# Conditioning groups as a low-priority stream on the Vector engine, own tables per layer, and token halves further apart in a two-layer diffusion trunk

## The chip, the cores and the metric

The kernel runs on one core of a Trainium2 chip. The metric is the device time of one execution in microseconds (us). A core has TensorE (PE; its weight loads are shown as PEld), VectorE (DVE), ScalarE (ACT), GpSimd (POOL) and SyncE (SP, which issues nearly all DMAs here). Each engine takes its instructions in the order in which the kernel wrote them.

## The reference, cut to what matters

Two layers over 256 latent tokens ("half 0", segment 0) and 256 context tokens ("half 1", segment 1), model width 1024, all in float32. The context is only an input to layer 1, so layer 1 computes half 0 alone in most places.

```python
for l in range(2):
    m  = silu(c)     @ ada_w[l] + ada_b[l]     # conditioning: 6 x 1024 for latent tokens
    mc = silu(c_ctx) @ ada_w[l] + ada_b[l]     # the same for context tokens
    h  = rms_norm(x, g0) * (1 + sc1) + sh1     # "modulate"
    y  = token_mix(h, hc, ...)                 # projection, branches A B C D, gated merge, out-projection w_o
    x  = x + g1 * rms_norm(y, g)               # "residual"
    h  = rms_norm(x, g2_) * (1 + sc2) + sh2
    x  = x + g2 * rms_norm(conv_ffn(h), g)     # up 1024 -> 2 x 2816, conv of width 3, gate, down
    # with l == 0 the same for the context: xc, hc, sh1c, ...
```

The merge is the sum over four branches of sigmoid(gate) * (branch @ w_br), then @ w_o.

## The kernel before

Every weight matrix is used in full float32 precision by splitting it into a high part in fp32r (a cast on ACT, `wh`) and a low part (a subtraction on DVE, `wl`); each product is three matmuls (high-high, high-low, low-high). `plan_layer` lists the weights in order, 1024 elements by 128 partitions each; `w_dma` loads them into NRAW raw buffers, `split_gen` splits them into NW pairs, `take` hands out the next, `drop` gives one back. A weight is 24 matmuls against 512 token columns, or against 256 where one half alone is computed.

Order: the program writes all engines' instructions in one order that a model of the engines' clocks decides on (`Model`, `Flow`). The main line writes TensorE's projections (`chunks`). After every three matmuls `Flow.poll` lets side generators write their next steps if what they wait for is ready by the model: first evacuations of results (`post`), then the norm chain of half 0 (`chain`), then splits of weights, then the streams in the order of STREAMS: `chain2` (norm chain of half 1), `pv`, `main` (attention, retention), `aux`, `fill` (convolution taps and tables). A stream takes a step only while DVE and ACT are, by the model, at most its limit ahead of TensorE (0.3 to 3 us). `Flow.until(cond)` polls until a condition holds; `idle_work` (conditioning on TensorE) is advanced only in such a loop. Waits in this order bind the order of instructions, not the engines: an engine on the chip waits only for data, buffers and what stands before it in its own queue.

PSUM has 8 banks; CAP says how many the main stream ("m"), scores and norms ("s"), transposes ("t") and retention or attention values ("v") may hold. Temporaries are 60 tiles (NT) of 128x512 float32 that all streams share.

Conditioning: each layer has 12 groups of 512 outputs (0, 1 shift; 2, 3 scale; 4, 5 gate; 6, 7 shift, 8, 9 scale, 10, 11 gate of the feed-forward). A group is made on TensorE (`ada_gen`: 8 loads of 256 KB, 8 products, 4 transposes, `adp`, `adt`) or on DVE (`ada_stream`: per 128 outputs two loads of 256 KB, and a multiply-and-reduce for each half of the 1024 inputs and each of the two vectors, `adw`, `adj`). Groups 0 to 3 of layer 0 run on TensorE at the start. Before the change the others were placed so: layer 0, groups 4 to 9 on DVE in stream `aux` beside the last merge (branch C), with all of `aux` written out before the out-projection; 10 and 11 on TensorE as idle work in the out-projection; layer 1, groups 0 and 2 as idle work before the feed-forward of layer 0, 1 and 3 on DVE in it, 4 to 6 as idle work in its last down-projection; 7 to 9 on DVE beside layer 1's last-but-one merge and the last, 10 and 11 as idle work in layer 1's out-projection.

Stages of layer 0 in the trace: projections and attention to 303 us, merge D 303 to 371, `proj_c` (projections of branch C) to 438, merge A with retention beside it to 529, merge C to 594, out-projection (`op`), feed-forward (`f`, `fa`, `fb`; down-projections also named `op`) from 677 to 1054. In `project` the last output chunks (`tail` of them) are computed for half 0 first and for half 1 after, with their weights held, so that half 0's norm chain (`residual`, `modulate`, tiles `rt`, `xs`, `q`, `ht`, `hh`, `hl`) runs under half 1's matmuls. The feed-forward then starts with four weights against half 0 and the same against half 1.

Of the kernel before, what the change touches and what calls it, by code (L numbers as in the profile page):

```python
# [8 lines left out]
F32 = mybir.dt.float32  # L9
# [6 lines left out]
KD = 8  # L16
# [128 lines left out]
class Flow:  # L145
# [7 lines left out]
    STREAMS = (("chain2", 3.0, 1), ("pv", 3.0, 1), ("main", 1.5, 2), ("aux", 1.5, 1), ("fill", 0.3, 1))  # L153
# [90 lines left out]
def trunk_kernel(  # L244
# [67 lines left out]
    CAP = {"m": 4, "s": 4, "t": 2, "v": 1}  # L312
# [22 lines left out]
    cst_sb = const.tile([128, 640], F32, name="cst_sb")  # L335
# [19 lines left out]
    CC = cst_sb[:, 384:512].rearrange("p (t d) -> p t d", t=2)  # L355
    SS = cst_sb[:, 512:640].rearrange("p (t d) -> p t d", t=2)
# [7 lines left out]
    ada = const.tile([128, 48, 2], F32, name="ada")  # L364
    gain = const.tile([128, 4, KD, 2], F32, name="gain")
    ada_next = const.tile([128, 16, 2], F32, name="ada_next")
    gain_next = const.tile([128, KD, 2], F32, name="gain_next")
# [42 lines left out]
    def tables_gen():  # L410
        yield (row_sb, vec_sb, cst_sb)
        act.copy(identr, ident)
        act.copy(masks, cst_sb[:, 128:384].rearrange("p (t d) -> p t d", t=2))
        for l in range(2):
            yield from layer_tables(l)
        finish_decays()
# [151 lines left out]
    def ada_gen(l, j, raw, nxt=False, h=None):  # L568
# [19 lines left out]
        o = (ada_next if nxt else ada)[:, c0:c0 + nc_, :]  # L588
# [8 lines left out]
        if idx is not None:  # L597
# [3 lines left out]
                out=(gain_next[:, ks, :] if nxt else gain[:, idx, ks, :]), in0=o,  # L601
# [5 lines left out]
    def c_rows_gen(vecs, rows_):  # L607

        for v in vecs:
            r = [tmp("crow") for _ in range(2)]  # L610
            for h in range(2):
                dma.dma_start(out=r[h], in_=c_b[:, v, 512 * h:512 * h + 512])
            rows_[v] = r
        for v in vecs:
            for h in range(2):
                t = rows_[v][h]
                yield (t,)
                th = tmp("crth")
                act.activation(out=th, in_=t, func=AF.Tanh, scale=0.5)
                yield (th,)  # L620
                dve.scalar_tensor_tensor(out=t, in0=th, scalar=1.0, in1=t, op0=ALU.add, op1=ALU.mult)

    def ada_stream(l, js, nxt=False, vecs=(0, 1)):

        A, G = (ada_next, gain_next) if nxt else (ada, gain)
        half_c = lambda c, h: ada_t[l, c, :, 512 * h:512 * h + 512]

        def load(c):
            r = [tmp("adw") for _ in range(2)]
            for h in range(2):  # L630
                dma.dma_start(out=r[h], in_=half_c(c, h))
            return r

        c_rows = {}
        yield from c_rows_gen(vecs, c_rows)
        cs = [4 * j + i for j in js for i in range(4)]
        raw = load(cs[0])
        for n_, c in enumerate(cs):
            cur, raw = raw, load(cs[n_ + 1]) if n_ + 1 < len(cs) else None
            for v in vecs:  # L640
                yield (cur[0], cur[1], c_rows[v][0], c_rows[v][1])
                a = small(1, "adc")
                for h in range(2):
                    junk = cur[h] if v == vecs[-1] else tmp("adj")
                    dve.tensor_tensor_reduce(
                        out=junk, in0=cur[h], in1=c_rows[v][h], scale=0.5,
                        scalar=(a if h else vec_sb[:, l, V_ADAB + c:V_ADAB + c + 1]), op0=ALU.mult, op1=ALU.add,
                        accum_out=(A[:, c, v:v + 1] if h else a),
                    )
                    yield  # L650
            if c % 4 == 3:
                c0 = c - 3
                kind, k0 = divmod(c0, 8)
                idx = {1: 0, 2: 1, 4: 2, 5: 3}.get(kind)
                w = slice(vecs[0], vecs[-1] + 1)
                if idx is not None:
                    ks = slice(k0, k0 + 4)
                    ng = vec_sb[:, l, V_NORM + 8 * idx + k0:V_NORM + 8 * idx + k0 + 4]
                    dve.scalar_tensor_tensor(
                        out=(G[:, ks, w] if nxt else G[:, idx, ks, w]), in0=A[:, c0:c0 + 4, w],  # L660
                        scalar=(1.0 if idx in (0, 2) else 0.0),
                        in1=ng.unsqueeze(2).to_broadcast([128, 4, len(vecs)]), op0=ALU.add, op1=ALU.mult,
                    )
                ada_done.update((l, x) for x in range(c0, c0 + 4))
# [34 lines left out]
    def new_S(name):  # L699
        return tp.tile([128, 256], F32, tag="S", name=name, bufs=4)  # L700
# [5 lines left out]

    def modulate(which, s, b, ks=range(KD), nxt=False):
        sh0 = (0, 24)[which]
        A, G = (ada_next, gain_next) if nxt else (ada, gain[:, (0, 2)[which]])
        R = b[:, 0:256]  # L710
        prev = None

# [1148 lines left out]
```

## Time and profile before

| | |
|---|---|
| time, median of 3 runs (lowest to highest) | 1666.54 us (1664.19 to 1669.51) |
| the profiled execution: its time, its span | 1664.61 us, 1662.8 us |
| busy share of the span: PE, DVE, ACT, POOL | 96%, 75%, 48%, 2% |
| mean granted TensorE clock | 0.978 of full speed |
| conditioning loads: `in_ada_w` (for TensorE), `in_ada_t` (for DVE) | 104 and 88 of 256 KB |

The span is the time from the first to the last instruction of one profiled execution. Busy is the time in which an engine executes; a matmul's end is modelled, so matmuls overlap in the record, and how fast they follow one another is read from their starts or from how many lie in a stretch. The clock is the share of full speed that the chip granted TensorE in a stretch; its two levels are 1.2 GHz (0.5) and 2.4 GHz (1.0). A releaser is the instruction whose end ended a wait.

### The profile page before, as it was taken

To read this page: it belongs to the slowest core of one execution; us is meant where nothing else is said; L and a number is where in the kernel's file an instruction comes from. 1 tells how busy PE (TensorE), PEld (TensorE's weight loads), DVE (VectorE), ACT (ScalarE), POOL (GpSimd) and SP (SyncE) were. 2 spreads that over 40 slices of the span, in tenths; PEclk is the share of its full clock that TensorE was granted. 3 is DMA by queue.
4 is the path that set the end of the run, shared out by engine and by line. 5 is a ranking of instruction groups with operands and counts; after the bars stand their busy time and mean duration, and the time that the engine had idled before them with its cause. 6 is when DMAs were issued, how large, how long until landed. Compare 5 with 4: busy or idle time off the path is not lost.

```text
span 1662.8 us, 25016 instructions
## 1 busy us (share of the span) xinstructions
PE 1603.9 (96%) x9358; PEld 1346.4 (81%) x9358; DVE 1245.9 (75%) x2698; ACT 793.0 (48%) x1705; POOL 36.5 (2%) x38
## 2 busy tenths in 40 slices
PE   6999999999999995899999999899999999999998
PEld 3876776788778875688888888788687999899998
DVE  4666898994585998799547546789887899578876
ACT  3666466324323314454334324456665554556653
POOL 0000000000000000000000000000100000000000
PEclk9999999999999997899999999899999999889999
DMA  9421211223313586254322326244133368626552
GB/s 337 153 64 39 76 64 51 76 89 99 111 55 122 190 290 244 76 170 160 101 94 96 102 82 220 82 149 139 52 117 116 118 208 283 245 90 217 183 173 73
DMA packets 83561, 224.80 MB, mean 135 GB/s; under 512 B 9073, under 2 KB 17777, under 8 KB 83441
## 3 DMA queue, kind: packets, MB, share of 16 engines
q1 hardware_dynamic: 83152, 222.69, 40.1%
q8 instruction: 73, 1.20, 0.3%
q10 hardware_dynamic: 288, 0.52, 0.1%
q14 instruction: 48, 0.39, 0.1%
HBM read 222.13 MB, written 1.05 MB: 134 GB/s over the span
## 4 chain that ended last, share of the span: by engine, by line
PE 77%; issue 13%; DVE 5%; DMA 3%; ACT 1%; SPq 0%; POOL 0%; POOLq 0%; DVEq 0%; ACTq 0%
PE mg L129 16%; PE tm L129 11%; PE op L129 9%; PE mb L129 8%; PE fa L129 7%; PE fb L129 7%; PE pv L129 3%; PE sc L129 2%; PE cqk L129 2%; PE pa L129 2%; PE ptp L129 2%; PE pg L129 2%; PE csc L129 1%; DVE adj L129 1%; PE nrm L129 1%
## 5 line engine op out<-in xcount | busy, mean ns | idle before, releaser
L129 DVE TENSOR_TENSOR wl<-raw,wh 128x512 fp32r<-128x512 f32 (+1 forms) x624 | 405.1, 680 | 152.1 <-ACT wh L129 151.0
L129 ACT CAST wh<-raw 128x512 fp32r<-128x512 f32 (+1 forms) x624 | 358.3, 613 | 174.7 <-PE fb L129 46.0
L129 PE MATMUL mg<-hh,wh 128*128 128x512 f32 (+1 forms) x512 | 178.8, 349 | 0.0
L129 PE MATMUL mg<-hh,wl 128*128 128x512 f32 (+1 forms) x512 | 172.3, 336 | 0.0
L129 PE MATMUL mg<-hl,wh 128*128 128x512 f32 (+1 forms) x512 | 172.3, 336 | 0.0
L129 DVE SCALAR_TENSOR_TENSOR co<-zp,hdw,co 128x482 f32<-128x482 f32 (+29 forms) x240 | 129.3, 602 | 0.0
L129 PE MATMUL op<-gh,wh 128*128 128x256 f32 (+1 forms) x370 | 122.2, 330 | 0.0
L129 PE MATMUL op<-gh,wl 128*128 128x256 f32 (+1 forms) x370 | 121.4, 328 | 0.0
L129 PE MATMUL op<-gl,wh 128*128 128x256 f32 (+1 forms) x370 | 121.4, 328 | 0.0
L129 PE MATMUL tm<-wh,hh 128*128 128x512 f32 x272 | 112.0, 412 | 2.8 <-ACT hh L129 2.8
L129 PEld LDWEIGHTS mg<-hh,wh 128*128 128x128 f32 x512 | 97.1, 190 | 20.3 <-issue 11.4
L129 ACT ACTIVATE mth<-mg 128x512 f32<-128x512 f32 (+1 forms) x64 | 31.5, 491 | 170.0 <-PE mg L129 169.5
L129 PE MATMUL tm<-wh,hl 128*128 128x512 f32 x272 | 107.0, 393 | 1.9 <-DVE hl L129 1.9
L129 PE MATMUL fa<-hh,wh 128*128 128x512 f32 (+1 forms) x320 | 107.6, 336 | 0.0
L129 PE MATMUL fa<-hl,wh 128*128 128x512 f32 (+1 forms) x320 | 107.5, 336 | 0.0
L129 PE MATMUL fa<-hh,wl 128*128 128x512 f32 (+1 forms) x320 | 107.5, 336 | 0.0
L129 PE MATMUL fb<-hh,wh 128*128 128x512 f32 (+1 forms) x320 | 107.5, 336 | 0.0
L129 PE MATMUL fb<-hl,wh 128*128 128x512 f32 (+1 forms) x320 | 107.5, 336 | 0.0
L129 PE MATMUL fb<-hh,wl 128*128 128x512 f32 (+1 forms) x320 | 107.5, 336 | 0.0
L129 PE MATMUL tm<-wl,hh 128*128 128x512 f32 x272 | 106.6, 392 | 0.0
L129 PEld LDWEIGHTS mg<-hh,wl 128*128 128x128 f32 x512 | 97.1, 190 | 10.2
L129 PEld LDWEIGHTS mg<-hl,wh 128*128 128x128 f32 x512 | 97.3, 190 | 8.1
(259 smaller groups left out, 3685.5 us busy)
## 6 DMA issues: line engine op xcount, KB each, us to landing
raw<-in_w_fm SPq DMA_DIRECT2D x88, 512.0 KB, 3.5
raw<-in_f_up SPq DMA_DIRECT2D x88, 512.0 KB, 3.7
adw<-in_ada_w SPq DMA_DIRECT2D x104, 256.0 KB, 5.4
adw<-in_ada_t SPq DMA_DIRECT2D x88, 256.0 KB, 5.2
raw<-in_w_tm SPq DMA_DIRECT2D x40, 512.0 KB, 3.5
raw<-in_w_br SPq DMA_DIRECT2D x32, 512.0 KB, 3.5
raw<-in_f_d SPq DMA_DIRECT2D x32, 512.0 KB, 3.5
raw<-in_w_o SPq DMA_DIRECT2D x16, 512.0 KB, 4.0
```

The lines of the kernel that those rows point to most:

```text
L129: r = f(*a, **kw)
```

## The change

The conditioning on DVE becomes a stream of its own, `ada`, last in STREAMS with a limit of 0.3 us. It has four sets, each of which begins when a stage is reached: layer 0, groups 4 and 5 from merge D on; layer 0, groups 6 to 9 from merge A on; layer 1, groups 0 to 3 and (latent vector alone) 6 to 9 from the feed-forward of layer 0 on. In a set all first halves of the chunks come first, then all second halves, which add to what the first left in the table. Each layer has its own tables `ada` and `gain`. The main line waits for groups 4 and 5 ahead of `proj_c`, for 6 to 9 after merge C and for layer 1's two sets ahead of the last down-projection. On TensorE remain groups 10 and 11 of both layers, all as idle work of layer 0's out-projection, and groups 4 and 5 of layer 1. `tail` is 5 instead of 3, the feed-forward of layer 0 starts with six weights (three pairs, LEAD) against half 0, the main stream may hold 6 banks, and six split and four raw weights are buffered instead of five and five. The space for it comes from smaller constants (masks are loaded to a temporary) and three instead of four tiles `S`.

```diff
-IN_MERGE = ((4, 5, 6, 7, 8, 9), (7, 8, 9))
-IDLE = (((10, 11), (4, 5, 6)), ((10, 11), ()))
+IDLE = ((((0, 10), (0, 11), (1, 10), (1, 11)), ((1, 4), (1, 5))), ((), ()))
+ADA_SETS = (
+    ("merge D", 0, (4, 5), (0, 1)), ("merge A", 0, (6, 7, 8, 9), (0, 1)),
+    ("ffn", 1, (0, 1, 2, 3), (0, 1)), ("ffn", 1, (6, 7, 8, 9), (0,)),
+)
-NRAW = 5
+NRAW = 4
-NW = 5
+NW = 6
+LEAD = 3
-    STREAMS = (..., ("aux", 1.5, 1), ("fill", 0.3, 1))
+    STREAMS = (..., ("aux", 1.5, 1), ("fill", 0.3, 1), ("ada", 0.3, 1))
-    CAP = {"m": 4, "s": 4, "t": 2, "v": 1}
+    CAP = {"m": 6, "s": 4, "t": 2, "v": 1}
-    ada = const.tile([128, 48, 2], F32, name="ada")
-    ada_next = const.tile([128, 16, 2], F32, name="ada_next")
+    ada = [const.tile([128, 48, 2], F32, name=f"ada{l}") for l in range(2)]
...
+        for when, l, js, vecs in ADA_SETS:
+            yield (lambda: when in stage,)
+            cs = [4 * j + i for j in js for i in range(4)]
+            for h in range(2):
+                rows_ = [tmp("crow") for _ in vecs]
+                for v, r in zip(vecs, rows_):
+                    dma.dma_start(out=r, in_=c_b[:, v, 512 * h:512 * h + 512])
+                raw = load(l, cs[0], h)
+                for r in rows_:
+                    yield (r,)
+                    th = tmp("crth")
+                    act.activation(out=th, in_=r, func=AF.Tanh, scale=0.5)
+                    yield (th,)
+                    dve.scalar_tensor_tensor(out=r, in0=th, scalar=1.0, in1=r, op0=ALU.add, op1=ALU.mult)
+                for n_, c in enumerate(cs):
+                    cur, raw = raw, load(l, cs[n_ + 1], h) if n_ + 1 < len(cs) else None
+                    for v, r in zip(vecs, rows_):
+                        yield (cur, r)
+                        o = ada[l][:, c, v:v + 1]
+                        dve.tensor_tensor_reduce(
+                            out=(cur if v == vecs[-1] else tmp("adj")), in0=cur, in1=r, scale=0.5,
+                            scalar=(o if h else vec_sb[:, l, V_ADAB + c:V_ADAB + c + 1]), op0=ALU.mult, op1=ALU.add,
+                            accum_out=o,
+                        )
...
-            tail = 3 if last and full else 0
+            tail = 5 if last and full else 0
...
+            stage.add("merge D")
             merge(stD)
+            flow.until(ada_need(0, 4, 5))
             proj_c()
...
+            stage.add("merge A")
             merge(stA, there=lambda: not flow.q["fill"])
             flow.drain("main")
-            go("aux", ada_stream(l, IN_MERGE[l]))
             merge(stC, last=True)
+            flow.until(ada_need(0, 6, 7, 8, 9))
         else:
-            go("aux", ada_stream(l, IN_MERGE[l], vecs=(0,)))
...
-            for j in (0, 2):
-                flow.idle_work.append(ada_gen(1, j, ada_load(1, j), nxt=True))
...
             chunks(list(zip(banks, ws)), H, L, half(0), KD, pre=lambda k: need(k, (0,)))
-            for p in range(2):
+            for _ in range(2):
+                banks.append(bank("m", "f0"))
+                ws.append(take(8))
+                chunks([(banks[-1], ws[-1])], H, L, half(0), KD)
+            for p in range(LEAD):
                 up_pair(p, banks[2 * p:2 * p + 2], ws[2 * p:2 * p + 2], half(1), pre=lambda k: need(k, (1,)))
...
-            go("aux", ada_stream(1, (1, 3), nxt=True))
+            stage.add("ffn")
...
+            flow.until(ada_need(1, 0, 1, 2, 3, 6, 7, 8, 9))
+            for i in IDLE[l][1]:
+                flow.idle_work.append(ada_gen(*i, ada_load(*i)))
         down(2, ys)
...
+    flow.add("ada", ada_stream())
```

## Rows read from the trace of the kernel before

**Rows 1.** The page's first part, and one of its costliest groups.

```profile
span 1662.8 us, 25016 instructions
...
PE 1603.9 (96%) x9358; PEld 1346.4 (81%) x9358; DVE 1245.9 (75%) x2698; ACT 793.0 (48%) x1705; POOL 36.5 (2%) x38
...
L129 DVE TENSOR_TENSOR wl<-raw,wh 128x512 fp32r<-128x512 f32 (+1 forms) x624 | 405.1, 680 | 152.1 <-ACT wh L129 151.0
```

**Rows 2.** TensorE's waits, 600 to 660: us in all, times, longest.

```profile
PE op L129 <- DVE wl L129: 12.6, 1, 12.6
PE op L129 <- ACT wh L129: 9.2, 1, 9.2
```

**Rows 3.** ACT's waits in the same stretch.

```profile
ACT ys L129 <- DVE adc L129: 30.6, 1, 30.6
```

**Rows 4.** Windows by stage: length, each engine's busy us, clock, DMA share, GB/s.

```profile
303.00:362.00 59.00, 59.00 (x262) 48.56 (x262) 57.29 (x91) 16.22 (x30) 0.00 (x0) 1.00 0.29 98
...
372.00:438.00 66.00, 66.00 (x299) 54.84 (x298) 28.56 (x45) 26.39 (x45) 0.00 (x0) 1.00 0.33 109
438.00:529.00 91.00, 91.00 (x450) 72.76 (x449) 62.53 (x147) 27.79 (x51) 4.40 (x4) 1.00 0.22 74
529.00:594.00 65.00, 65.00 (x288) 53.81 (x288) 56.40 (x124) 24.01 (x43) 0.00 (x0) 1.00 0.59 195
594.00:621.00 27.00, 27.00 (x121) 22.36 (x120) 25.74 (x68) 1.77 (x3) 0.00 (x0) 1.00 0.92 330
621.00:644.00 23.00, 1.26 (x5) 0.54 (x3) 22.39 (x65) 8.15 (x19) 0.00 (x0) 0.56 0.56 207
...
715.00:802.00 87.00, 87.00 (x385) 72.08 (x384) 83.95 (x159) 41.69 (x70) 0.00 (x0) 1.00 0.48 158
802.00:1020.00 218.00, 218.00 (x963) 180.56 (x963) 114.88 (x176) 80.22 (x138) 0.00 (x0) 1.00 0.29 94
...
1438.00:1458.00 20.00, 16.06 (x88) 10.87 (x86) 12.19 (x34) 7.02 (x17) 2.37 (x2) 0.71 0.31 105
```

**Rows 5.** The same windows for tile `adw` alone: PE, PEld, DVE.

```profile
529.00:594.00 65.00, 0.00 (x0) 0.00 (x0) 26.46 (x36) 1.00 0.59 195
594.00:644.00 50.00, 0.00 (x0) 0.00 (x0) 42.92 (x60) 0.80 0.76 273
```

**Rows 6.** DVE's timeline, 600 to 606: start, us, instruction.

```profile
602.20 0.75 DVE L129 CUSTOM_DVE_ANT_0 adw<-adw,crow,vec_sb 128x512 f32<-128x512 f32 x1
...
602.99 0.75 DVE L129 CUSTOM_DVE_ANT_0 adw<-adw,crow,adc 128x512 f32<-128x512 f32 x1
...
603.67 0.75 DVE L129 CUSTOM_DVE_ANT_0 adj<-adw,crow,vec_sb 128x512 f32<-128x512 f32 x1
```

**Rows 7.** The chain of work, 360 to 380: start, us, what.

```profile
371.72 0.89 PE abc L129 x8
...
375.36 0.89 PE abc L129 x8
```

**Rows 8.** The chain of work around layer 0's feed-forward turn and its end.

```profile
644.02 12.38 PE op L129 x88
656.40 0.34 PE nrm L129 x4
...
664.19 0.35 PE nrm L129 x4
...
699.62 15.08 PE f L129 x96
...
1050.72 2.87 PE op L129 x24
```

**Rows 9.** TensorE's timeline, 674 to 679.

```profile
676.78 0.39 PE L129 MATMUL f<-hh,wh 128*128 128x256 f32 x1 [1.12 <-ACT hh L129]
```

**Rows 10.** TensorE's timeline, 1051 to 1074.

```profile
1053.86 1.07 PE L129 MATMUL adp<-adw,cS 128*32 128x512 f32 x8
...
1070.04 0.66 PE L129 MATMUL adt<-cst_sb,adsb 128*128 128x128 f32 x4 [2.28 <-ACT adsb L129]
...
1072.88 0.56 PE L129 MATMUL pg<-hh,wh 128*128 128x256 f32 x1
```

**Rows 11.** ACT's timeline, 1042 to 1075.

```profile
1065.12 0.91 ACT L129 ACTIVATE hh<-ht,ada_next 128x256 fp32r<-128x256 f32 x2 [3.02 <-DVE ht L129]
```

More of the change, by code (lines that the diff above doesn't have):

```diff
@@ L145 @@
 class Flow:
-    STREAMS = (("chain2", 3.0, 1), ("pv", 3.0, 1), ("main", 1.5, 2), ("aux", 1.5, 1), ("fill", 0.3, 1))
+    STREAMS = (("chain2", 3.0, 1), ("pv", 3.0, 1), ("main", 1.5, 2), ("aux", 1.5, 1), ("fill", 0.3, 1), ("ada", 0.3, 1))
     def __init__(self, model):
@@ L363, in trunk_kernel @@
     hh, hl = [None] * KD, [None] * KD
-    ada = const.tile([128, 48, 2], F32, name="ada")
-    gain = const.tile([128, 4, KD, 2], F32, name="gain")
-    ada_next = const.tile([128, 16, 2], F32, name="ada_next")
-    gain_next = const.tile([128, KD, 2], F32, name="gain_next")
+    ada = [const.tile([128, 48, 2], F32, name=f"ada{l}") for l in range(2)]
+    gain = [const.tile([128, 4, KD, 2], F32, name=f"gain{l}") for l in range(2)]
     def pair(name, shape):
@@ L412, in tables_gen @@
         act.copy(identr, ident)
-        act.copy(masks, cst_sb[:, 128:384].rearrange("p (t d) -> p t d", t=2))
+        mk = raw_masks.pop()
+        yield (mk,)
+        act.copy(masks, mk.rearrange("p (t d) -> p t d", t=2))
         for l in range(2):
@@ L600, in ada_gen @@
             dve.scalar_tensor_tensor(
-                out=(gain_next[:, ks, :] if nxt else gain[:, idx, ks, :]), in0=o,
+                out=gain[l][:, idx, ks, :], in0=o,
                 scalar=(1.0 if idx in (0, 2) else 0.0),
@@ L623, in ada_stream @@
[L623 to L664, printed above, removed]
@@ new lines, in trunk_kernel, with ada_stream, load @@
+    stage = set()
+    def ada_stream():
+        def load(l, c, h):
+            t = tmp("adw")
+            dma.dma_start(out=t, in_=ada_t[l, c, :, 512 * h:512 * h + 512])
+            return t
+        for when, l, js, vecs in ADA_SETS:
+            yield (lambda: when in stage,)
+            cs = [4 * j + i for j in js for i in range(4)]
+            for h in range(2):
+                rows_ = [tmp("crow") for _ in vecs]
[18 more added lines that the diff above has]
+                        )
+                    if h and c % 4 == 3:
+                        c0 = c - 3
+                        kind, k0 = divmod(c0, 8)
+                        idx = {1: 0, 2: 1, 4: 2, 5: 3}.get(kind)
+                        w = slice(vecs[0], vecs[-1] + 1)
+                        yield
+                        if idx is not None:
+                            ks = slice(k0, k0 + 4)
+                            ng = vec_sb[:, l, V_NORM + 8 * idx + k0:V_NORM + 8 * idx + k0 + 4]
+                            dve.scalar_tensor_tensor(
+                                out=gain[l][:, idx, ks, w], in0=ada[l][:, c0:c0 + 4, w],
+                                scalar=(1.0 if idx in (0, 2) else 0.0),
+                                in1=ng.unsqueeze(2).to_broadcast([128, 4, len(vecs)]), op0=ALU.add, op1=ALU.mult,
+                            )
+                        ada_done.update((l, x) for x in range(c0, c0 + 4))
@@ L705, in need, with modulate @@
         flow.until(lambda: all((s, k) in hready for s in segs))
-    def modulate(which, s, b, ks=range(KD), nxt=False):
+    def modulate(l, which, s, b, ks=range(KD)):
         sh0 = (0, 24)[which]
-        A, G = (ada_next, gain_next) if nxt else (ada, gain[:, (0, 2)[which]])
+        A, G = ada[l], gain[l][:, (0, 2)[which]]
         R = b[:, 0:256]
@@ L733, in modulate, with residual @@
         rest(*prev)
-    def residual(which, s, ys, b, Sx=None, sums=None):
+    def residual(l, which, s, ys, b, Sx=None, sums=None):
         R = b[:, 0:256]
@@ L768, in residual @@
             dve.scalar_tensor_tensor(
-                out=t, in0=ys[k][:, half(s)], scalar=gain[:, (1, 3)[which], k, s:s + 1], in1=R,
+                out=t, in0=ys[k][:, half(s)], scalar=gain[l][:, (1, 3)[which], k, s:s + 1], in1=R,
                 op0=ALU.mult, op1=ALU.mult,
@@ L787, in norm_chain @@
             b2 = bank("s", "nrm")
-            yield from residual(which, s, ys, b, sums=b2)
+            yield from residual(l, which, s, ys, b, sums=b2)
             added.add((l, which))
@@ L795, in norm_chain @@
             yield
-            yield from residual(which, s, ys, b, Sx)
+            yield from residual(l, which, s, ys, b, Sx)
             free(b)
@@ L1442, in final_feature @@
                 u = half_tmp("fu")
-                dve.tensor_scalar(out=u, in0=y, scalar1=gain[:, 3, m, 0:1], scalar2=None, op0=ALU.mult)
+                dve.tensor_scalar(out=u, in0=y, scalar1=gain[l][:, 3, m, 0:1], scalar2=None, op0=ALU.mult)
                 if m < KD - 1:
@@ L1694, in layer @@
             for p in range(p0, p0 + nk):
-                if p > 1:
+                if p >= (LEAD if full else 2):
                     up_pair(p)
@@ L1731, in start_chain @@
             yield (lambda: {(0, c) for c in (k, k + 1, 8 + k, 9 + k)} <= ada_done,)
-            yield from modulate(0, s, b, (k, k + 1))
+            yield from modulate(0, 0, s, b, (k, k + 1))
         free(b)
-    first = []
+    first, raw_masks = [], []
     for j, h in ((0, 0), (0, 1), (1, 0), (1, 1)):
```

38 lines of the change are left out of this document (12 added, 26 removed).

## The prediction

> **What bounds the kernel now.** I read the page's first part, then TensorE's waits, then the windows by stage, then the chain of waits and the timelines around the few places where TensorE stops. TensorE is busy 1603.9 of 1662.8 us [rows 1], so everything but TensorE's own stream is hidden, and a gain can only come from three sources: stretches where TensorE waits, stretches where it runs at the lower clock, and work that can be taken off it. One wait is large: in the out-projection of layer 0 it stands 9.2 us for a cast of ACT and then 12.6 us for a low half of DVE [rows 2]. ACT's own queue says why: a copy of the projection's result stood 30.6 us behind DVE's conditioning [rows 3], because its buffer came from that work, and the casts of weights stood behind that copy. The window 621 to 644 shows it: TensorE 1.26 of 23 us, DVE 22.39, clock 0.56 [rows 4]. The stage before it shows where it comes from: the conditioning of layer 0, groups 4 to 9, is 96 reduce instructions on DVE (24 chunks, 2 vectors, 2 halves), started with merge C at 529; 36 of them were through at 594, when that merge ended, and 60 came after it [rows 4, 5]. From 594 TensorE ran exactly the weights that were split ahead (5 x 5.44 = 27.2 us, at 87.00 us for 385 matmuls or 226 ns each, 24 to a weight [rows 4]), then stood.
>
> The smaller places are the turns from one sublayer to the next, where half 0 of the tokens goes through residual, norm and modulation while TensorE holds some half-1 work to cover it. Out-projection to feed-forward: half 0 ends near 656, half 1 near 664, the first matmul on new rows is at 676.8, the first on half 1 at 699.6 [rows 8, 9]. Layer 0 to 1: half 1 ends near 1053.9, the first `pg` comes at 1072.9 [rows 10]. Layer 1's own turn: 1438 to 1458 at clock 0.71 [rows 4].
>
> **The change, part by part.** The sum is against the profiled run (span 1662.8, 1664.61 us in all); the median shown is 1.9 us above that run, and I carry the difference over.
>
> *The stall after merge C (T1).* Groups 4 and 5 now go from merge D on, 6 to 9 from merge A on. The second set is 64 reduces. One that reads the accumulator just written starts 0.79 us after its predecessor, one that doesn't starts 0.68 after (602.20, 602.99, 603.67 [rows 6]). With the first halves of all chunks before the second halves none reads a fresh one, so the set is 64 x 0.68 = 43.5, and 46.2 with four preparations of vector rows, each the size of a weight's low half (0.68 [rows 1]). The room: DVE is idle 91 - 62.5 = 28.5 us in merge A and, without the 26.46 us of its 36 reduces, 65 - (56.4 - 26.5) = 35 us in merge C [rows 4, 5]. 46.2 into 63.5 goes, even at the last place in line; what is left at the end lies under six weights (32.6 us) instead of five. So the 21.8 us go: T1 = -21.8, between -21.8 and -8 (if the whole 46.2 came after the merge: 46.2 - 32.6 = 14 stay). After the wait, 88 matmuls took 12.38 us [rows 8] against 88 x 0.120 = 10.6 (24 in 2.87 [rows 8]) at the lower clock: T2 = -1.8, or 0.
>
> *Half 0 earlier (T3, T4).* Five of eight output chunks are split by halves instead of three: half 0 ends 2 x 24 x 0.120 = 5.8 us sooner against half 1, and the cover grows from 8.6 to 14.4 us. In the feed-forward six weights instead of four run on half 0 first, 17.3 instead of 11.5 us. First matmul after half 0's end: 676.8 - 656.4 = 20.4; first on half 1: 43.2 after it [rows 8, 9]. Both count from half 0, as half 1's residual stands in DVE's queue behind half 0's. Before, from the end of half 1 to the end of three pairs: 35.4 to 699.6, 15.1 for four half-1 weights (96 matmuls [rows 8]; 11.5 at full clock), then the third pair 10.9: 61.4. After: 43.2 - 14.4 = 28.8, then 17.3 for six half-1 weights, so 46. TensorE's own work in that stretch, though, is 34.6 + four conditioning groups of 2.7 (8 products in 1.07 us, two such runs and 0.66 of transposes [rows 10]) + some 4 of small products = 49.4, which is the floor. I take 51: T3 = -10, between -12 and -4 (half 1 bound by its own end: 35.4 + 17.3 + a group or two).
> At the turn of the layers the first rows were done some 20 us after half 0's end (1053.9 - 8.6 = 1045.3; ACT's first `hh` at 1065.1 [rows 11]), now 20 - 14.4 = 6 us after half 1's. But TensorE came to `pg` only at 1072.9, as the transposes of three conditioning groups, waiting 2.28 us and more on ACT, lay ahead [rows 10]. One group less and 5.8 us more cover: half 1's end to `pg` falls from 19 us to the 9 or 10 that two groups and the small products take. T4 = -8 (0 to -11; 0 if the transposes still come last).
>
> *Three groups off TensorE.* By the lists TensorE keeps 6 groups besides the first four, of 9 (I count three moved, not four), and DVE has 192 reduces, of 152. The first is within T4. The other two leave layer 1's turn with their 16 loads of 256 KB: the chain there had products of these groups between its own. T5 = -4, between -6 (their 5.4 us and more) and +3.6. Against it stands the clock: that stretch was at 0.71 even with them [rows 4], and with less to do TensorE may stay at the lower level further into the feed-forward. At the other turn such a start cost 15.08 us for 96 matmuls [rows 8] against 11.5, and those 3.6 are the upper end. The Trainium skill, "TensorE: Matmul & The Clock Gate", section "What's actually happening", goes that way: the lowered clock is the default, and activity lifts it, so filler work has a value. By that rule alone T5 would be +3.6, and the sum 7.6 us higher; the trace agrees in that the clock is low where TensorE has gaps, and no row here shows this turn without filler.
>
> *The new stream in the feed-forward.* 96 reduces and six preparations, 69 us. DVE is idle 87 - 84 = 3 and 218 - 115 = 103 us there, the old 32 reduces included in the busy time [rows 4]; TensorE is full throughout. Cost 0, hidden by the feed-forward's matmuls; uncovered, the 64 reduces more would be 43 us, which the 103 idle us exclude.
>
> *The forced end after merge D (T6).* Here the change adds a wait to the order: conditioning groups 4 and 5 must be emitted before `proj_c`. Convolution taps fill DVE until 362 (57.3 of 59 us [rows 4]) and stand ahead of the new stream, so nearly all of this set, 32 x 0.68 + 2.8 = 24.6 us, comes into DVE's queue behind merge D. Behind it stand the splits of weights and the tail of the convolution. TensorE's instructions of `proj_c` don't wait for conditioning itself. Ahead of them, however, now stands the second `abc` product, which ran 3.6 us after the first [rows 7], between matmuls of `proj_c`: lower end +3.5. DVE's queue from 372 is some 12 (the 28.56 us it does until 438 [rows 4] less 12 weights' splits of two halves) + 24.6 + six splits of 1.36 = 45 us; with six weights split ahead TensorE has work until 376 + 32.6 and then waits some 8 us, less what it gets sooner. With none split ahead it waits for all of the set: 3.5 + 24.6 = 28, the upper end. Merge C is the nearest case, and there the weights split ahead were used to the last, so I stay near the lower end: T6 = +5.
>
> *The 32 loads at the out-projection* (8.4 MB, before 16) stand on SP ahead of later weights: at the 330 GB/s of 594 to 621 [rows 4] 25 us, hidden by ten weights loaded ahead (54 us of matmuls): 0, and up to those 25 if they were not. Four buffers for raw weights plus six split are ten as before: 0. Tables and smaller constants: 0.
>
> Sum: -21.8 - 1.8 - 10 - 8 - 4 + 5 = -40.6. 1664.6 - 40.6 = 1624, and 1626 against the median.
>
> **Rivals.** *The stall moves to merge D.* DVE takes its instructions in the order written, so "low priority" in the list is none on the chip, and the splits may stand behind the 24.6 us. For: the stall of today is just that [rows 2, 3]. Against: splits are asked for before the streams. T6 = +28: 1649. *The further halves buy nothing*, since DVE's and ACT's chain, not cover, is what lasts: T3 and T4 are 0: 1644. *The stream starves*: last in line with the tightest limit, it gets nothing in merge A and C, and 14 us of stall stay: 1640. *Slower: PSUM.* TensorE's main stream may hold six of eight banks instead of four, and a score step of attention takes two. Where DVE frees banks late, attention starves, and the drain after merge B ends later. Attention runs beside full projections now, so no row shows a wait on banks; it decides once attention costs more than the 41 us won; at 49 it gives 1675. Against: a unit of merge holds two banks, and DVE would have to be a unit of 8 us late.
>
> **Numbers.** Forecast 0.60 (alone 1615 to 1641), stall at merge D 0.15, halves 0.11, starved 0.06, banks 0.08. What a measurement here can tell from no change is about 0.3%, 5 us. All but the banks and the far end of the second are faster: faster 0.90, within 0.04, slower 0.06. The range: T1 to T5 at their best with T6 at its least give 1664.6 - 49 = 1616, 1617 by the median; five more for terms set at 0, 1612. Above it takes in the first two rivals: 1650.
>
> **What would show it.** T1: no wait of TensorE over 3 us between the end of merge C and the out-projection's last chunk, and the last reduce of layer 0 before that merge ends or within 10 us. T2: clock 1.00 there. T3: three pairs done some 51 us after the half-1 end. T4: `pg` about 10 us after it. T5: first `f` of layer 1 within 17 us of the last `op`. T6: at the start of `proj_c` a gap of 3 to 8 us in all, and the reduces of groups 4 and 5 all after the last tap. Wrong would make it: a gap over 20 us there, or TensorE idle in attention.

## The result, and the profile after

The changed kernel takes 1646.57 us (median; 1645.5 to 1650.32), the kernel before on the same chip 1666.88: a ratio of 0.988, 95% interval 0.986 to 0.991. That is 1.2% faster, with the interval clear of 1, and inside the range of 1612 to 1650, but 20 us of gain stand where 40 were forecast. The page of the profiled run after answers to [rows 1]:

```profile
span 1645.3 us, 25202 instructions
...
PE 1594.7 (97%) x9430; PEld 1349.9 (82%) x9430; DVE 1273.9 (77%) x2774; ACT 796.5 (48%) x1712; POOL 36.6 (2%) x38
...
L136 DVE TENSOR_TENSOR wl<-raw,wh 128x512 fp32r<-128x512 f32 (+1 forms) x624 | 403.7, 679 | 106.9 <-ACT wh L136 105.6
```

The stall is gone. TensorE's waits from 600 to 660 (us in all, times, longest) no longer hold the two rows of [rows 2]:

```profile
PE f L136 <- ACT hh L136: 1.1, 1, 1.1
PE nrm L136 <- POOL nr L136: 1.0, 1, 1.0
```

The windows by stage (columns as in [rows 4]) and the same for tile `adw` alone (as [rows 5]) show why:

```profile
374.00:445.00 71.00, 67.82 (x296) 55.81 (x295) 52.13 (x114) 27.41 (x47) 0.00 (x0) 0.98 0.49 163
445.00:538.00 93.00, 92.19 (x452) 73.16 (x451) 81.15 (x202) 29.58 (x53) 4.93 (x4) 1.00 0.35 118
538.00:603.00 65.00, 65.00 (x289) 53.81 (x288) 51.68 (x108) 22.88 (x41) 0.00 (x0) 1.00 0.49 166
603.00:630.00 27.00, 27.00 (x164) 24.23 (x163) 15.83 (x38) 10.53 (x24) 0.00 (x0) 1.00 0.92 328
630.00:653.00 23.00, 23.00 (x198) 22.30 (x196) 11.24 (x28) 10.74 (x27) 0.70 (x1) 1.00 0.55 198
```

```profile
374.00:445.00 71.00, 0.00 (x0) 0.00 (x0) 23.23 (x32) 0.98 0.49 163
445.00:538.00 93.00, 0.00 (x0) 0.00 (x0) 18.93 (x27) 1.00 0.35 118
538.00:603.00 65.00, 0.00 (x0) 0.00 (x0) 21.70 (x30) 1.00 0.49 166
603.00:653.00 50.00, 0.72 (x8) 0.16 (x8) 6.10 (x9) 1.00 0.75 268
```

All 32 reduces of groups 4 and 5 lie in the branch-C projections; of 6 to 9 most lie beside merges A and C, and the few left in the out-projection (a reduce that crosses an edge is counted on both sides) lie under the six split weights: TensorE works through at clock 1.00.

To find the missing 20 us I cut both traces at the same instructions. Most stretches keep their length to 0.1 us from kernel to kernel where the same work stands in them, so a difference points to a place. Two don't: the branch-C projections with unchanged work took 70.4 to 71.7 us over these kernels, layer 1 up to its out-projection 340.7 to 345.1. Lengths in us, from TensorE's timelines:

| from ... to the first product of | before | after | change |
|---|---|---|---|
| start ... merge B | 193.93 | 195.26 | +1.3 |
| ... branch-C projections | 176.95 | 179.17 | +2.2 |
| ... merge A | 67.13 | 70.42 | +3.3 |
| ... out-projection | 156.09 | 157.83 | +1.7 |
| first to last product of the out-projection | 70.09 | 49.67 | -20.4 |
| last half-1 product ... fourth pair | 61.25 | 57.53 | -3.7 |
| ... end of the last half-1 product of layer 0 | 328.15 | 331.43 | +3.3 |
| ... layer 1 (`pg`) | 19.29 | 13.21 | -6.1 |
| ... its out-projection | 341.88 | 343.17 | +1.3 |
| ... its feed-forward | 43.73 | 43.58 | -0.2 |
| ... its last product | 197.56 | 197.05 | -0.5 |

Start to merge B holds nearly the same instructions in every kernel of this study and took 193.8 to 196.8 us, so its 1.3 tells nothing.

Three places in the timeline after explain most. At the start of the branch-C projections (answering to [rows 7]) one weight comes late; first TensorE's row, then DVE's rows before it:

```profile
410.75 0.79 PE L136 MATMUL tm<-wl,hh 128*128 128x512 f32 x1 [3.18 <-DVE wl L136]
```

```profile
397.88 0.74 DVE L136 CUSTOM_DVE_ANT_0 adj<-adw,crow,ada 128x512 f32<-128x512 f32 x1
...
398.67 0.75 DVE L136 CUSTOM_DVE_ANT_0 adw<-adw,crow,ada 128x512 f32<-128x512 f32 x1
...
399.34 0.75 DVE L136 CUSTOM_DVE_ANT_0 adj<-adw,crow,ada 128x512 f32<-128x512 f32 x1
...
410.01 1.29 DVE L136 TENSOR_TENSOR wl<-raw,wh 128x512 fp32r<-128x512 f32 x2
```

From 376 to 410 DVE splits no weight at all. The six split ahead carry TensorE to 407.6, then it waits 3.18 us.

At the out-projection's turn (as [rows 8, 9]) TensorE's timeline has conditioning products both ahead of the first rows of half 1 and after them:

```profile
676.31 2.78 PE L136 MATMUL adp<-adw,cS 128*32 128x512 f32 x24
679.55 1.07 PE L136 MATMUL adp<-adw,cS 128*32 128x512 f32 x8 [0.45 <-ACT adsb L136]
680.54 0.61 PE L136 MATMUL nrm<-ones,Sx 128*128 128x1 f32 x4
681.08 1.06 PE L136 MATMUL adp<-adw,cS 128*32 128x512 f32 x8
682.93 0.66 PE L136 MATMUL adt<-cst_sb,adsb 128*128 128x128 f32 x4 [0.78 <-ACT adsb L136]
683.42 0.61 PE L136 MATMUL nrm<-cst_sb,nr 128*128 128x128 f32 x4
685.14 0.39 PE L136 MATMUL f<-hh,wh 128*128 128x256 f32 x1 [1.11 <-ACT hh L136]
...
705.80 1.03 PE L136 MATMUL adt<-cst_sb,adsb 128*128 128x128 f32 x8
706.77 1.92 PE L136 MATMUL adp<-adw,cS 128*32 128x512 f32 x16
709.47 0.65 PE L136 MATMUL adt<-cst_sb,adsb 128*128 128x128 f32 x4 [0.78 <-ACT adsb L136]
709.88 0.49 PE L136 MATMUL fa<-hh,wh 128*128 128x512 f32 x1
```

The first half-1 row is used at 685.14, 32.8 us after the last half-1 product at 652.35. The products of one idle group and the transposes of three come only behind the half-1 weights, so the fourth pair starts 4 us later than the rows would allow. The groups ahead also hold up half 1's own norm chain, whose two products `nrm` stand behind them in TensorE's queue: DVE had ended the sum `Sx` at 679.48, 1.1 us before its product at 680.54, and POOL its `nr` at 682.12, 1.3 us before the product at 683.42.

At the turn of the layers (as [rows 10, 11]) TensorE's and ACT's timelines show the last group's transposes still ahead of `pg`, their copy behind the eight modulations:

```profile
1047.98 0.66 PE L136 MATMUL adt<-cst_sb,adsb 128*128 128x128 f32 x4
1049.19 0.71 PE L136 MATMUL nrm<-cst_sb,nr 128*128 128x128 f32 x4 [0.56 <-POOL nr L136]
1053.76 1.11 PE L136 MATMUL adt<-cst_sb,adsb 128*128 128x128 f32 x4 [3.86 <-ACT adsb L136]
1054.52 0.56 PE L136 MATMUL pg<-hh,wh 128*128 128x256 f32 x1
```

```profile
1047.27 0.91 ACT L136 ACTIVATE hh<-ht,ada 128x256 fp32r<-128x256 f32 x2 [0.46 <-DVE ht L136]
...
1053.14 0.56 ACT L136 COPY adsb<-adp 128x512 f32<-128x512 f32 x1
```

### The profile page after: what moved, and what is told of

It reads as the page before. It is cut to its first block, busy times and chain, and to the rows that moved or that the text cites. A ratio compares the mean times of both kernels' runs of the same rounds, so it can differ in the third digit from the quotient of the medians.

```text
span 1645.3 us, 25202 instructions
## 1 busy us (share of the span) xinstructions
PE 1594.7 (97%) x9430; PEld 1349.9 (82%) x9430; DVE 1273.9 (77%) x2774; ACT 796.5 (48%) x1712; POOL 36.6 (2%) x38
## 3 DMA queue, kind: packets, MB, share of 16 engines
HBM read 223.18 MB, written 1.05 MB: 136 GB/s over the span
## 4 chain that ended last, share of the span: by engine, by line
PE 78%; issue 13%; DVE 5%; DMA 2%; ACT 1%; POOL 0%; SPq 0%; DVEq 0%; POOLq 0%; ACTq 0%
PE mg L136 16%; PE op L136 11%; PE tm L136 11%; PE mb L136 8%; PE fa L136 6%; PE fb L136 6%; PE pv L136 3%; PE sc L136 2%; PE pg L136 2%; PE pa L136 2%; PE ptp L136 2%; PE f L136 2%; PE cqk L136 1%; PE co L136 1%; PE csc L136 1%
## 5 line engine op out<-in xcount | busy, mean ns | idle before, releaser
L136 PE MATMUL fa<-hh,wh 128*128 128x256 f32 (+1 forms) x312 | 104.6, 335 | 0.0
L136 PE MATMUL fa<-hh,wl 128*128 128x256 f32 (+1 forms) x312 | 104.4, 335 | 0.0
L136 PE MATMUL fa<-hl,wh 128*128 128x256 f32 (+1 forms) x312 | 104.4, 335 | 0.0
L136 PE MATMUL fb<-hh,wh 128*128 128x256 f32 (+1 forms) x312 | 104.4, 335 | 0.0
L136 PE MATMUL fb<-hl,wh 128*128 128x256 f32 (+1 forms) x312 | 104.4, 335 | 0.0
L136 PE MATMUL fb<-hh,wl 128*128 128x256 f32 (+1 forms) x312 | 104.4, 335 | 0.0
L136 ACT ACTIVATE mth<-mg 128x512 f32<-128x512 f32 (+1 forms) x64 | 31.4, 490 | 150.2 <-PE mg L136 149.8
```

Source lines behind the costliest of these rows:

```text
L136: r = f(*a, **kw)
```

## The experiments

Each kernel was timed beside the kernel before; ratios are to it, with 95% intervals. The kernel after stands at 0.988. Stretches are those of the table.

**e1, halves back.**

```diff
-            tail = 5 if last and full else 0
+            tail = 3 if last and full else 0
...
-LEAD = 3
+LEAD = 2
...
-            for _ in range(2):
-                banks.append(bank("m", "f0"))
-                ws.append(take(8))
-                chunks([(banks[-1], ws[-1])], H, L, half(0), KD)
```

> The kernel after, with the token halves as far apart as before (three chunks computed by halves instead of five, feed-forward started with four weights on half 0 instead of six); all of the conditioning stays as changed. Theory H (the halves' gain was real and something else ate it; terms T3 and T4 of the prediction as sized, -18): 1658 to 1664 us. Theory O (half 1's norm chain counts from its own end, and the layer turn's end is set by conditioning transposes, so the further halves gave little net): 1645 to 1650 us, and from the last half-1 matmul of the out-projection to the first feed-forward matmul on half 1 about 33 us, as in the kernel after (32.8).

1653.5 us, 0.993 (0.992 to 0.995): 8.7 us slower than after by the ratios, 6.9 by the median times, 6.4 by the spans of the traces. Neither theory holds: the halves are worth half of what I gave them, not all and not nothing. The out-projection takes 52.53 us instead of 49.67, last half-1 product to fourth pair 61.57 instead of 57.53, to `pg` 17.33 instead of 13.21. But the stretch between is 328.15 again, 3.3 us shorter: with five halved chunks the small norm products of half 0 stand between half-1 products and push them back (the last section has the sizes).

**e17, lead back.** The kernel after with only LEAD 2 and four weights on half 0.

> The kernel after with the feed-forward started with four weights on half 0 instead of six, the five halved chunks kept. Theory V (half 1's rows come some 33 us after its last product whatever TensorE does, so the work that TensorE has on half 0 in that stretch is what counts: two weights, 5.8 us): 1650 to 1653 us. Rival (the further halving of the out-projection gave the 8.7 us, and the lead nothing): 1645 to 1648 us.

1646.14 us, 0.989 (0.987 to 0.990): the lead earned nothing, theory V is wrong. Its timeline shows why; TensorE after the four half-0 weights:

```profile
671.15 5.36 PE L136 MATMUL adp<-adw,cS 128*32 128x512 f32 x48
676.87 0.66 PE L136 MATMUL adt<-cst_sb,adsb 128*128 128x128 f32 x4 [0.36 <-ACT adsb L136]
677.46 1.06 PE L136 MATMUL adp<-adw,cS 128*32 128x512 f32 x8
678.46 1.09 PE L136 MATMUL adt<-cst_sb,adsb 128*128 128x128 f32 x8
```

The idle groups fill the place of the two weights, all of them ahead of half 1's first row (684.3, 31.4 us after the last half-1 product). Last half-1 product to fourth pair is 57.69 against 57.53. Lead and groups compete for one stretch; the halved chunks earned what there was. What the lead would earn without the groups was not tried.

**e4 and e9, e7: groups 10 and 11 of layer 1 out of this turn.** In e4 they join the feed-forward's stream on DVE; in e9 they are a DVE set of their own that begins with layer 1's first merge and that the main line waits for after its last; in e7 they are TensorE's idle work in layer 1's out-projection.

```diff
-IDLE = ((((0, 10), (0, 11), (1, 10), (1, 11)), ((1, 4), (1, 5))), ((), ()))
+IDLE = ((((0, 10), (0, 11)), ((1, 4), (1, 5))), ((), ()))
...
# e4
-    ("ffn", 1, (6, 7, 8, 9), (0,)),
+    ("ffn", 1, (6, 7, 8, 9, 10, 11), (0,)),
...
# e9
+    ("merges 1", 1, (10, 11), (0,)),
...
# e7
-        for i in IDLE[l][0]:
+        for i in IDLE[l][0] if l == 0 else ((1, 10), (1, 11)):
```

> The kernel after, but groups 10 and 11 of layer 1 are made on the Vector engine in the first feed-forward (latent vector alone, 16 reduces more there) instead of on TensorE in the out-projection of layer 0. Theory P (their products come after the first three pairs and lie on the path: 4.2 us there, 5.4 of TensorE in all): 1641 to 1643 us. Rival (they fill stretches in which TensorE would wait for half 1's rows): 1645 to 1647 us, the time appearing as a longer wait for half 1's rows.

> The kernel after, but groups 10 and 11 of layer 1 are made on the Vector engine beside layer 1's merges (latent vector alone, 16 reduces). Theory P (in layer 0's out-projection turn these groups lie on TensorE's path): from the last half-1 product to the end of three pairs 51 us instead of 57.5, and 1638 to 1641 us. Rival (16 reduces more beside the merges of layer 1 hold up weights there, or the groups were cover): 1644 us or more, with waits for low halves between 1300 and 1420.

> The kernel after, but groups 10 and 11 of layer 1 are idle work on TensorE in layer 1's out-projection again, as before the change, instead of in layer 0's. Layer 0's turn gains some 6.4 us in each case (as in the run with these groups on the Vector engine, from the last half-1 product to the end of three pairs 51 us instead of 57.5). What layer 1's turn does tells three theories apart. Term T5 as predicted (their absence there was worth 4 us): 1643 us, the interval from the first out-projection product of layer 1 to its first feed-forward product 4 us longer than the 43.6 of the kernel after. The clock rule (filler is worth 3.6 us there): 1635 us. What the two traces suggest (it makes no difference): 1639 us, interval 43.6 as before and after.

In all three the stretch to the fourth pair falls to 51.1, 51.7 and 51.1 us, the value that theory P gives: two groups cost 6 us there, more than their 5.4 of products. Of the 6.4 in e7, 4.1 are the work behind the half-1 weights, which is gone, and 2.3 are half 1's rows, which come 30.5 us after its last product instead of 32.8. What came of it differs. e4: 1649.4 us, 0.991 (0.989 to 0.992), as the feed-forward lost 7.7 us (339.12 to its last half-1 product). e9: 1643.07, 0.986 (0.985 to 0.988), two more us lost beside layer 1's merges. e7: 1640.03, 0.984 (0.983 to 0.986): all kept, and layer 1's turn not longer but 1.05 us shorter (42.53).

**e8 and e3, e13: groups 4 and 5 of layer 1 off TensorE at the turn of the layers.** In e3 they are made on DVE in the feed-forward's stream, in e13 the same with the stream's limit at 1.5 us, in e8 as a set beside layer 1's merges, as in e9.

```diff
# e3, e13
-    ("ffn", 1, (6, 7, 8, 9), (0,)),
+    ("ffn", 1, (4, 5, 6, 7, 8, 9), (0,)),
...
# e13
-    STREAMS = (..., ("ada", 0.3, 1))
+    STREAMS = (..., ("ada", 1.5, 1))
...
# e8
+    ("merges 1", 1, (4, 5), (0,)),
```

> The kernel after, but groups 4 and 5 of layer 1 are made on the Vector engine in the first feed-forward (latent vector alone, 16 reduces more there), so that TensorE has no conditioning at the turn from layer 0 to 1. Theory Q (the turn's end is set by the last group's four transposes, whose copy stands behind eight modulations in ScalarE's queue): first matmul of layer 1 some 7 us after the last half-1 matmul instead of 13.4, 1638 to 1641 us. Rival C (the modulation chain itself or a lower clock without filler sets the end): 1644 to 1648 us, with a longer wait for rows of half 0 or a granted clock below that of the kernel after in the 30 us behind the turn.

> The kernel after, but groups 4 and 5 of layer 1 are made on the Vector engine beside layer 1's merges (latent vector alone, 16 reduces), so that TensorE has no conditioning at the turn of the layers and the feed-forward's stream is as in the kernel after. Theory Q (the last group's transposes set the turn's end; the earlier run lost it again because its reduces were written in one block ahead of the last down-projection and half 0's sum of squares came late): first matmul of layer 1 some 8 us after the last half-1 product instead of 13.2, nothing lost in the down-projection, 1639 to 1642 us. Rival C (without filler the clock or the chain takes it back): 1644 to 1648 us with the granted clock at the turn lower than after's for over 10 us.

> The run with layer 1's groups 4 and 5 in the feed-forward's stream once more, with one number changed: the stream may be 1.5 us ahead of TensorE by the model instead of 0.3. Theory L (the limit starves the stream, which leaves 16 reduces to be written in one block ahead of the last down-projection although the Vector engine is idle a quarter of the time): last reduce before 1000 us, no wait of TensorE for half 0's sum of squares in the down-projection, 1639 to 1642 us. Rival (the room is used up, whatever the limit): the block stays, or waits appear in the feed-forward, 1647 us or more.

The turn itself is 8.19 us in all three instead of 13.21, as theory Q says. e8: 1640.59 us, 0.985 (0.983 to 0.987). e3: 1650.19, 0.991 (0.990 to 0.992), slower than after although its turn is 5 us shorter. Its down-projection shows where it went: 16 reduces come between 1000.4 and 1020.8, 13 of them one after another from 1010.3 on, and half 0's sum of squares behind them. First the answer for tile `adw` on DVE from 1000 to 1030, then TensorE's row:

```profile
L136 DVE CUSTOM_DVE_ANT_0 adw<-adw,crow,ada x16: 746/748/753, 1000.4 to 1020.8; 128x512 f32<-128x512 f32 x16
```

```profile
1035.32 1.01 PE L136 MATMUL nrm<-ones,Sy 128*128 128x1 f32 x4 [3.50 <-DVE Sy L136]
```

e13: 1642.49 us, 0.986 (0.985 to 0.988), with the last reduce at 973.3, no such wait and 331.42 us where e3 has 338.21. DVE had the room; the limit of 0.3 us kept the stream from using it.

**e2, no forced end.**

```diff
-            flow.until(ada_need(0, 4, 5))
             proj_c()
...
-            flow.until(ada_need(0, 6, 7, 8, 9))
+            flow.until(ada_need(0, 4, 5, 6, 7, 8, 9))
```

> The kernel after, but the main line no longer waits for groups 4 and 5 of layer 0 ahead of the branch-C projections; it waits for them together with 6 to 9 after merge C. Theory F (the forced end writes 34 us of reduces into the Vector engine's queue without a weight split, and TensorE's 3.2 us wait, the slow clock after it and the bunched products are its price, 5.5): 1641 us, the wait for the low half gone, first product of merge A 4 to 6 us earlier. Rival (the same reduces come a little later and hold up other weights, in merge A or at the out-projection): 1645 to 1648 us.

1639.27 us, 0.985 (0.984 to 0.986). Merge B to merge A takes 177.01 and 67.13 us, what it took before, and merge A to the out-projection 0.9 less than after: theory F, and next to nothing came back later (the stretch to the fourth pair is 57.95 instead of 57.53).

**e6, late sets.** With the wait of e2, and:

```diff
-            stage.add("merge D")
...
-            stage.add("merge A")
             merge(stA, there=lambda: not flow.q["fill"])
             flow.drain("main")
+            stage.add("merge D")
+            stage.add("merge A")
```

> The kernel after, but layer 0's two sets (groups 4 to 9) begin only with merge C, as before the change, and the main line waits for them after that merge alone. Theory S (term T1: the early start is what removed the stall): the 60 or so reduces that don't fit beside merge C keep the Vector engine 49 us before it can split again, as before; six split weights cover 32.6 of it instead of 27.2, so TensorE stands some 16 us in the out-projection and runs slow for 2 after it; with the 5.5 us of the forced end ahead of the branch-C projections gone: 1656 to 1660 us. Rival (the sixth split weight, the halves or the new order of the reduces removed it): no wait over 4 us there, 1640 to 1643 us.

1680.61 us, 1.009 (1.007 to 1.010): the stall is back, and larger than I expected. TensorE's waits, 596 to 690:

```profile
PE op L136 <- ACT wh L136: 35.2, 1, 35.2
PE op L136 <- DVE wl L136: 2.4, 1, 2.4
```

At the last place in line only 24 of the 96 reduces got into merge C (36 before the change), so 72 stood ahead of the splits. The out-projection takes 89.73 us instead of 49.67. So it is the early start that pays, not the low priority or the sixth weight.

**e15, buffers back.** e1 with four banks and five and five weights (`CAP` m 4, NRAW 5, NW 5).

> The run with the halves as before (1653.5 us), and besides it the buffers as before: four PSUM banks for the main stream, five raw and five split weights. The prediction's zero for buffers: 1651 to 1656 us. Rival (the sixth split weight covers what is left of the reduces after merge C): 1657 to 1661 us, with a longer wait in layer 0's out-projection.

1654.49 us, 0.994 (0.992 to 0.995), like e1, though not for want of effects: with five split weights the wait at the branch-C projections is 8.6 us instead of 3.2 (one weight is 5.4), and the out-projection, with no wait for half 0's sum of squares (3.5 us in e1), is 6.6 us shorter. The zero held as a sum only.

**e12, e16, e14: together.** e12 is e2, e7 and e8 in one; e14 the same with `out=tmp("adj")` for every reduce; e16 is e2, e7 and e13.

> The kernel after with three edits together: no forced end ahead of the branch-C projections (alone -5.5), groups 10 and 11 of layer 1 on TensorE in layer 1's out-projection (alone -6), groups 4 and 5 of layer 1 on the Vector engine beside layer 1's merges (alone -5.5). If the three are independent places of loss, as the traces suggest: 1627 to 1631 us. If one covers another (the out-projection's turn of layer 1 now carries both the late reduces and the two groups): 1633 to 1638 us.

> The three edits together, and the second vector's reduce writes its unused products to a buffer of its own instead of over its input. Theory W (a reduce that overwrites the tile which the reduce before it reads starts late: 0.79 us after it instead of 0.67): 0.67 us for both kinds, the set of 64 reduces 4 us shorter, time as without it within 2 us, as the Vector engine isn't the bound. Rival (the 0.79 comes from the neighbouring column of the table): 0.79 stays.

> No forced end ahead of the branch-C projections, groups 10 and 11 of layer 1 in layer 1's out-projection on TensorE, and groups 4 and 5 of layer 1 in the feed-forward's stream with the limit of 1.5 us (instead of beside layer 1's merges, as in the three together). Theory R (the 4 us that the three together lacked of their sum were the reduces beside layer 1's last merge, which held up its norm chain): first out-projection product of layer 1 to its first feed-forward product 42.5 us instead of 47.8, 1626 to 1629 us. Rival (the turn of layer 1 is longer whatever the reduces do): 1631 to 1634 us, interval over 46.

e12: 1632.21 us, 0.980 (0.979 to 0.982), between its two figures. e16: 1628.47, 0.978 (0.977 to 0.980), the fastest here: theory R. Layer 1's turn, TensorE's timeline, first of e12, then of e16:

```profile
1402.08 2.78 PE L136 MATMUL adp<-adw,cS 128*32 128x512 f32 x24
1407.68 0.61 PE L136 MATMUL nrm<-ones,Sy 128*128 128x1 f32 x4 [2.81 <-DVE Sy L136]
```

```profile
1402.14 2.78 PE L136 MATMUL adp<-adw,cS 128*32 128x512 f32 x24
1404.85 0.60 PE L136 MATMUL nrm<-ones,Sy 128*128 128x1 f32 x4
```

In e12 the sum of squares `Sy` comes 2.8 us late, and the whole turn, 47.81 against 42.53, follows it. Theory R puts that down to the reduces beside layer 1's last merge, but they alone don't do it: in e8, with the same 16 reduces and no groups on TensorE in this turn, the product of `Sy` starts 25.5 us after the out-projection's first, as in the kernel after (28.7 in e12). The traces show what the two do together. The 16 loads of the groups, `in_ada_w`, are written behind the wait for those reduces, and the next weight's load stands behind them on SP. In e12 it is issued at 1397.02, in e16, without the reduces, at 1387.81. First SP's, then ACT's timeline of e12:

```profile
1384.24 12.38 SPq L136 DMA_DIRECT2D adw<-in_ada_w  x16
1397.02 3.19 SPq L136 DMA_DIRECT2D raw<-in_f_up  x4
```

```profile
1402.97 1.14 ACT L136 CAST wh<-raw 128x512 fp32r<-128x512 f32 x2 [3.29 <-DMA raw<-in_f_up]
```

The cast waits for that load, and the square that `Sy` needs stands behind the cast in ACT's queue.

e14: 1633.53, 0.981 (0.980 to 0.982), as fast as e12; its reduces are told of below.

## Why the prediction was half right

**T1 and T2 (-23.6): right.** The stall and the slow clock after it are gone, the out-projection is 20.4 us shorter. The 3 us between I put down to half 0's small products and the halved chunks, which now lie in this stretch: with three halved chunks and no stall it takes 45.96 (e15). e6 shows the early start as the cause. The size of the set was read too low: its reduces stand 0.73 us apart on average and not 0.68 (last section), some 3 us for 64, which stayed hidden.

**T3 (-10, at least -4): wrong, -3.7, and the step that failed is its 51 us.** I had half 1's first row 28.8 us after its last product, since half 1's residual stood "in DVE's queue behind half 0's". It came 32.8 us after it; 35.4 before and in e1, 31.4 in e17. Its residual counts from half 1's own end, the case that I had named as the upper bound: it begins 14.5 us after half 1's last product before and 14.4 after, but 22 and 31 us after half 0's last. DVE's timeline, before and then after (half 1's last product ends at 664.19 and 652.35):

```profile
678.74 0.87 DVE L129 SCALAR_TENSOR_TENSOR rt<-ys,gain,nrm 128x256 f32<-128x256 f32 x2
```

```profile
666.71 0.88 DVE L136 SCALAR_TENSOR_TENSOR rt<-ys,gain,nrm 128x256 f32<-128x256 f32 x2 [1.78 <-PE nrm L136]
```

And I added four groups into a floor of 49.4 as if they fitted into gaps. They don't: with two of them the stretch is 51.1 (e7), with four 57.5. That 57.5 is 32.8 to the rows, 20.7 for the six half-1 weights instead of 17.3, at a mean clock of 0.92, and 4.1 of groups behind them. Of the 3.4 more, by the starts of the matmuls, some 1.3 are spacing at the lower clock and some 2 longer gaps among the first 30 of 144; e7, with two groups, has the same. There were four groups in this turn before as well, 0 and 2 of layer 1 in place of 10 and 11; the floor counted their products, but not that they come behind the rows and hold them up. The six leading weights, half of the edit, earned nothing beside these groups (e17). That the forecast of 51 is what e4 and e7 measure with two groups is luck: its parts were others.

**T4 (-8, 0 if the transposes still come last): -6.1 in the turn, but -2.8 with what paid for it.** They did come last; without the two groups the turn is 8.19 (e8), where 9 or 10 had been forecast with them. And the stretch before it grew by 3.3 us (e1: by nothing), since half 0's norm products now interrupt half 1's matmuls (some 2.7 us) and two more chunks run by halves (some 0.6). The norm products are not new work: before, they lay in the turn. I counted the growth of the cover and not that the chain's own products move into it.

**T5 (-4): wrong, -0.2 in the turn.** Two groups less there saved nothing, and putting them back makes the turn 1.05 us shorter (e7). Layer 1 has no second half to cover the chain. The windows of this turn (columns as in [rows 4]), of the kernel after and then of e7:

```profile
1420.90:1441.30 20.40, 11.83 (x49) 10.32 (x49) 12.07 (x29) 6.59 (x16) 1.77 (x2) 0.59 0.32 114
```

```profile
1415.40:1434.70 19.30, 14.90 (x89) 10.48 (x86) 12.72 (x35) 7.73 (x18) 1.78 (x2) 0.76 0.35 120
```

The groups fill time in which TensorE waited, and the granted clock is 0.76 with them instead of 0.59. The direction is that of the rule which the prediction had weighed against its own sum, the Trainium skill, "TensorE: Matmul & The Clock Gate", section "What's actually happening": activity releases the lowered clock. The price is not the 3.6 us that I gave it but 1, and it is shown for e7's order alone: before, with the same two groups in this turn, it took 43.73, not less than without them, and why is open.

**T6 (+5): right, 5.5**, at the place and by the mechanism forecast: 2.2 for the `abc` products ahead of the projections (3.5 forecast), 3.3 for the wait and the slow clock after it; without the forced end both are gone (e2).

**The zeros.** The feed-forward's stream cost nothing as changed, but at the edge of what its limit lets through: 16 reduces more cost 7 us (e3, e4). Beside merges A and C the reduces cost 1.7 us, 0.9 of it due to the forced end (e2). Layer 1's projections and merges took 1.3 us more; over these kernels they took 340.7 to 345.1 with the order of their side work, and I did not take that apart.

In sum: of the 23 us between -40.6 and -17.5, T3 is 6.3, T4 with the growth ahead of it 5.2, T5 with layer 1's end 3.3, T1 and T2 3.2, T6 0.5, and the places set at nothing 4.4, the start among them. The rival "the further halves buy nothing" was nearest in time (1644), and half right: the chain lasts, but halving chunks still gave 6 to 9 us.

Not tried: the kernel before with the early start alone.

## What to carry to other kernels

Work that "fills idle time" has to be placed by the gap that it fills: the same two groups cost 6 us in a turn that was already covered and were worth 1 in one that wasn't. A low-priority stream needs a limit that lets it use the idle time, because what it leaves is written in one block at the point where it is due, ahead of a chain that ends a stage. And when a chain gets more cover, count its own instructions into the cover, and ask from which event the other chain starts before shortening the first.

## What the runs showed of the hardware

A reduce that overwrites the tile which the reduce just before it reads starts 0.79 us after it, other neighbours in this kernel 0.67 us apart (the three rows of 397 to 399 above). In the kernel before no reduce does that, and 0.79 stood where one reads the accumulator just written (602.20 and 602.99 of [rows 6]), as the prediction has it: either costs the same 0.12. So the order by halves, which I expected to give 0.68 throughout, took away one of the two and brought in the other, and gave 0.73 on average. Where no reduce writes in place (e14), the gap is 0.67 between two in a row:

```profile
371.92 0.74 DVE L136 CUSTOM_DVE_ANT_0 adj<-adw,crow,vec_sb 128x512 f32<-128x512 f32 x1
...
372.60 0.75 DVE L136 CUSTOM_DVE_ANT_0 adj<-adw,crow,vec_sb 128x512 f32<-128x512 f32 x1
```

The time did not change (e14 beside e12). The small norm products cost TensorE more than their one column of output suggests: each row of four (128x1) between matmuls of the down-projection moved the next matmuls on by some 0.45 us. Six more such rows stand there after than before, 2.7 of the 3.3 us; the rest, by estimate, are the two more chunks run by halves, at two times 2.87 us [rows 8] where a whole one takes 5.44.
